# Outer products of a two-stream feed-forward block by seven block products, with two of the four weight sums made by accumulating DMAs

## The chip, the cores and the metric

The kernel runs on one core of one Trainium2 chip. The metric is the time of one execution on the device in microseconds (us), the median of a few runs. One further execution was taken by the hardware profiler, and all rows of a trace here are from that one. TensorE is called PE, VectorE DVE, ScalarE ACT, GpSimd POOL, SyncE SP.

## What is computed

The reference runs a first block (two layers of branches and a convolved feed-forward on `x`, 256 tokens of 1024), and then a second block of two layers on two streams, `x` and a context `c` of 256 tokens each. The change is in the second block's feed-forward half-steps:

```python
def modulate(h, m, i):
    return h * (1.0 + m[:, 3 * i + 1][:, None]) + m[:, 3 * i][:, None]

def ffn_half_step(s, m, i, norm_g, w_in, w_out):
    h = modulate(rmsnorm(s, norm_g), m, i)
    gu = h @ w_in
    y = (jax.nn.silu(gu[..., :D_FF]) * gu[..., D_FF:]) @ w_out
    return s + 0.5 * gate(m, i) * y
...
for l in range(DEPTH):
    m_x = modulation(c, w_mod[l], b_mod[l])
    m_c = modulation(c_ctx, w_mod[l], b_mod[l])[None]
    xs = ffn_half_step(xs, m_x, 0, ffn1_norm[l], ffn1_w_in[l], ffn1_w_out[l])
    cs = ffn_half_step(cs, m_c, 0, ffn1_norm[l], ffn1_w_in[l], ffn1_w_out[l])
    ...
    xs = ffn_half_step(xs, m_x, 2, ffn2_norm[l], ffn2_w_in[l], ffn2_w_out[l])
    if not last:
        ...
        cs = ffn_half_step(cs, m_c, 2, ffn2_norm[l], ffn2_w_in[l], ffn2_w_out[l])
```

Both streams go through the same weights, with D_FF = 2816. So three of the four half-steps work on two streams; the last one (layer 1, second half-step) on `x` alone. Between the half-steps of a layer lies a mixer with latent attention. The modulation is a product of a condition vector with 72 columns of 128 per layer.

## The kernel before, in words

All is float32. A matrix product is made of three float32r matmuls: each operand is split into a high part (a cast on ACT, L298) and the rest (a subtraction on DVE, L299), and `mm3` (L303 to L305) adds high by high, high by low and low by high into one PSUM bank. Tokens are the columns of a matmul (512 for both streams, 256 for one), weights are the stationary 128x128.

`ffn2` is a half-step. D_FF is cut into KF = 22 column blocks `j` of 128. For each, gate and up are made from one 512 KB weight tile each (8 blocks of the inner dimension, `times`), then silu and product, and the split of the result into an `r4` tile `g`. It works in two halves of 11 column blocks: after each half the down projection runs over the 8 output columns `d`, with one weight tile of 6 blocks (384 KB) and one of 5 (320 KB), and `gated_add` (L1086) adds the result, times the modulation's gate, to the residual `xs` or `cs`.

To start a half-step without waiting for its norm, the kernel makes the first column pairs from operands without the root: `ahead` (L1041, L1042) splits the residual times gain column by column as the gated additions finish, `firsts` multiplies them (and a 2-column bias, hence 258 columns), and `rooted` (L1067, L1070) multiplies the result by the root R afterwards. Layer 0's first half-step does this otherwise: there `h2` prepares the context ahead, and `first_two` makes its first pair. `streams` makes h from R for the remaining column blocks (two three-operand forms a block and stream, L1013 and L1016).

The modulation is made on DVE: `mod_step` loads a column block of its weights into `wm` (512 KB, two buffers) and multiplies it by the condition (L468, one for each stream). The products are kept in a queue `self.mods`; the calls `mod_step(n)` take n of them at a place in the program, and `mod_in`, `mod_out` are deadlines, which take all that a half-step's gains (or gates) need. In `ffn2` the calls stand behind the gate and up products and the loads of the down projection.

Loads are issued by SP. Buffers: `raw` 4 of 1024, `whi` and `wlo` 4 each, `r4` 15, `r4b` 4, PSUM 4 banks `ps`, 2 `sc`, 2 `tp`. The order within an engine comes from the tile framework that builds the program; each engine runs its own in order.

In the profile the names of tiles begin with the phase: `dn` in layer 0's first half-step of the second block, `lat` to `wa` in the mixer, `wo` from the mixer's output projection on and in the half-steps behind it.

## Time and profile before

| | before |
|---|---|
| median of 3 runs | 2477.66 us (2476.97 to 2477.69) |
| profiled execution | 2476.86 us |
| its span, first to last instruction | 2475.1 us |
| PE busy | 2456.9 us (99%), mean granted clock 0.999 |
| DVE busy | 1812.9 us (73%), 3180 instructions |
| ACT busy | 1197.4 us (48%), 2084 instructions |
| POOL busy | 1.2 us, 14 instructions |
| DMA | 395.91 MB, mean 160 GB/s |

A busy share is an average over the whole span. The section of rows below shows the same in slices and in windows; a row of a timeline gives the start, the duration, the engine, the line, and what the engine waited for before it. Instructions on DVE and ACT overlap by some 0.08 us, so that the distance between two starts, not the duration, is what an instruction takes of its engine.

### The profile page before, as it was taken

How to read it: one execution, taken by the hardware profiler on the slowest of the kernel's cores; microseconds unless marked ns; L12 is line 12 of the kernel's file. 1: busy time of each engine (PE TensorE's matmuls, PEld its weight loads, DVE VectorE, ACT ScalarE, POOL GpSimd, SP SyncE). 2: the span in 40 equal slices, each digit the busy share in tenths (PEclk: the TensorE clock that was granted, in tenths of full speed). 3: DMA queues.
4: the chain of work that ended last, by engine and by line, in shares of the span. 5: the costliest groups of instructions: out<-in, count | busy, mean ns of one | idle time of the engine just before them, and what ended most of it. 6: DMA issues, size and time to landing. Idle time of an engine off the chain costs nothing.

```text
span 2475.1 us, 39396 instructions
## 1 busy us (share of the span) xinstructions
PE 2456.9 (99%) x15211; PEld 2170.2 (88%) x15211; DVE 1812.9 (73%) x3180; ACT 1197.4 (48%) x2084; POOL 1.2 (0%) x14
## 2 busy tenths in 40 slices
PE   8999999999999999999999999999999999999998
...
DVE  8888887988998886776757875655765643688654
...
GB/s 251 172 156 181 199 183 235 183 152 172 216 215 205 202 197 149 211 182 125 115 59 42 120 147 127 177 145 125 123 147 163 244 153 74 91 117 139 178 206 120
DMA packets 123851, 395.91 MB, mean 160 GB/s; under 512 B 14352, under 2 KB 17168, under 8 KB 123408
## 3 DMA queue, kind: packets, MB, share of 16 engines
...
HBM read 392.30 MB, written 1.05 MB: 159 GB/s over the span
## 4 chain that ended last, share of the span: by engine, by line
PE 95%; DVE 2%; ACT 1%; DMA 0%; issue 0%; SPq 0%; DVEq 0%; ACTq 0%
PE wops L305 13%; PE wops L303 13%; PE wops L304 13%; PE dnps L304 6%; PE dnps L305 6%; PE dnps L303 6%; PE upps L305 3%; PE upps L303 3%; PE upps L304 3%; PE qkvps L304 1%; PE qkvps L305 1%; PE qkvps L303 1%; PE cvps L303 1%; PE cvps L305 1%; PE cvps L304 1%; PE latps L304 1%
## 5 line engine op out<-in xcount | busy, mean ns | idle before, releaser
L298 ACT CAST wowhi<-woraw 128x1024 fp32r<-128x1024 f32 (+3 forms) x266 | 246.4, 928 | 581.9 <-PE wops L304 359.6
L305 PE MATMUL wops<-wor,wowlo 128*128 128x512 f32 (+2 forms) x1371 | 480.5, 351 | 0.0
L303 PE MATMUL wops<-wor,wowhi 128*128 128x512 f32 (+2 forms) x1371 | 478.9, 350 | 0.0
L304 PE MATMUL wops<-wor,wowhi 128*128 128x512 f32 (+2 forms) x1371 | 478.6, 349 | 0.0
L299 DVE TENSOR_TENSOR wowlo<-woraw,wowhi 128x1024 fp32r<-128x1024 f32 (+3 forms) x266 | 283.9, 1071 | 216.9 <-ACT wowhi L298 208.7
L304 PEld LDWEIGHTS wops<-wor,wowhi 128*128 128x128 f32 x1371 | 258.0, 188 | 38.0 <-DVE wor L1042 0.2
L305 PEld LDWEIGHTS wops<-wor,wowlo 128*128 128x128 f32 x1371 | 257.9, 188 | 36.5
L303 PEld LDWEIGHTS wops<-wor,wowhi 128*128 128x128 f32 x1371 | 257.5, 188 | 36.5
L298 ACT CAST dnwhi<-dnraw 128x768 fp32r<-128x768 f32 (+2 forms) x144 | 125.1, 871 | 290.7 <-PE dnps L304 184.6
L299 DVE TENSOR_TENSOR dnwlo<-dnraw,dnwhi 128x768 fp32r<-128x768 f32 (+2 forms) x144 | 143.8, 1000 | 69.5 <-ACT dnwhi L298 66.9
L305 PE MATMUL upps<-hr,upwlo 128*128 128x256 f32 x656 | 183.2, 280 | 1.5 <-DVE upwlo L299 1.5
L304 PE MATMUL upps<-hr,upwhi 128*128 128x256 f32 x656 | 183.9, 281 | 0.0
L303 PE MATMUL upps<-hr,upwhi 128*128 128x256 f32 x656 | 183.8, 280 | 0.0
L468 DVE SCALAR_TENSOR_TENSOR dnjunk<-dnwm,cond 128x1024 bf16<-128x1024 f32 x134 | 163.5, 1220 | 2.9 <-DMA dnwm<-in_wm 1.7
L305 PE MATMUL dnps<-dnr,dnwlo 128*128 128x512 f32 (+1 forms) x371 | 142.4, 384 | 0.0
L304 PE MATMUL dnps<-dnr,dnwhi 128*128 128x512 f32 (+1 forms) x371 | 142.2, 383 | 0.0
L303 PE MATMUL dnps<-dnr,dnwhi 128*128 128x512 f32 (+1 forms) x371 | 142.1, 383 | 0.0
L468 DVE SCALAR_TENSOR_TENSOR wojunk<-wowm,cond 128x1024 bf16<-128x1024 f32 x114 | 138.9, 1219 | 0.0
L305 PEld LDWEIGHTS upps<-hr,upwlo 128*128 128x128 f32 x656 | 123.2, 188 | 2.3 <-DVE upwlo L299 2.3
L303 PEld LDWEIGHTS upps<-hr,upwhi 128*128 128x128 f32 x656 | 123.6, 188 | 0.0
L304 PEld LDWEIGHTS upps<-hr,upwhi 128*128 128x128 f32 x656 | 123.1, 188 | 0.0
L1127 DVE TENSOR_TENSOR wof<-wof,wops 128x512 f32<-128x512 f32 (+1 forms) x59 | 35.5, 602 | 110.2 <-PE wops L305 110.2
...
## 6 DMA issues: line engine op xcount, KB each, us to landing
woraw<-in_w2u SPq DMA_DIRECT2D x132, 512.0 KB, 3.7
upraw<-in_w1u SPq DMA_DIRECT2D x82, 512.0 KB, 4.3
wowm<-in_wm SPq DMA_DIRECT2D x73, 512.0 KB, 4.4
dnwm<-in_wm SPq DMA_DIRECT2D x67, 512.0 KB, 4.2
dnraw<-in_w2u SPq DMA_DIRECT2D x44, 512.0 KB, 4.2
...
woraw<-in_w2d SPq DMA_DIRECT2D x48, 320.0 KB, 2.9
qkvraw<-in_w1q SPq DMA_DIRECT2D x24, 512.0 KB, 4.4
```

The source lines that it names most:

```text
L298: act = self.nc.scalar.copy(hi, src)
L299: return act, self.nc.vector.tensor_tensor(lo, src, hi, ALU.subtract)
L303: mm(ps, L[0], R[0], start=st, stop=False)
L304: mm(ps, L[0], R[1], start=False, stop=False)
L305: mm(ps, L[1], R[0], start=False, stop=sp)
L468: nc.vector.scalar_tensor_tensor(junk, self.wm, 1.0, self.cond[:, s, :], ALU.mult, ALU.mult, accum_out=self.M[l][s][step][:, j:j + 1])
L1127: nc.vector.tensor_tensor(s, s, pss[1], ALU.mult)
```

## The change

The three half-steps on two streams go from `ffn2` to a new `ffn2s`; `ffn2` keeps the last one. In `ffn2s` two column blocks are made by `firsts` and `rooted`, in layer 0's first half-step too (`ahead` now prepares both streams there). The other 20 are made by seven products in Strassen's manner (Winograd's form): for one column block the matrix of weights has two rows, gate and up, and two halves of the inner dimension, and the matrix of activations has these halves and the two streams. `sums` makes seven activation operands once per half-step. `seven` makes seven weight operands of 4 blocks each. Each of the seven products is 4 blocks x 3 matmuls of 256 columns, 84 in all, where 48 of 512 columns stood.

Two of the four sums of weights are additions on DVE (L1161). The others are accumulating DMAs from HBM, issued by POOL: `es` is first loaded with half of up (SP), and the other half is added to it; gate's first half is added to the raw up tile. Each moves 256 KB; there are 120.

The down projection runs over three chunks of 8, 7 and 7 column blocks (`CHUNKS`), with one weight tile of 1024 or 896 a column, so that there are three rounds of `gated_add`. The modulation products stand elsewhere: one per column block from the seventh on, `mod_gate` per output column in the first chunk, two per column in the second, one in the third, and new calls in the mixer: one or two behind each product of `proj`, and one per output column of its projections (`mix2`). `r4b` has 8 buffers, `es` 2 of 1024, and `rope2`, `K2` and `Q2` live in `r4b` tiles.

```diff
-NU = {(0, 2): 2, (1, 0): 2, (1, 2): 3}
+NU = 2
+CHUNKS = ((0, 8), (8, 15), (15, 22))
...
+    def sums(self, Rs, more):
...
+        def h(out, s, k):
+            nc.vector.scalar_tensor_tensor(out, X[s][:, k, :], self.A[s][:, k:k + 1], Rs[s], ALU.mult, ALU.mult)
+            nc.scalar.activation(out, out, AF.Identity, bias=self.B[s][:, k:k + 1])
...
+        for k in range(4):
...
+            h(c1, 1, k)
+            h(f[:, T:], 1, k + 4)
+            nc.vector.tensor_tensor(t3, f[:, T:], c1, ALU.subtract)
+            h(f1[:, :T], 0, k)
+            nc.vector.tensor_tensor(f1[:, T:], f1[:, :T], c1, ALU.subtract)
+            two(f1, "x1", "t1")
+            nc.vector.scalar_tensor_tensor(f[:, :T], f1[:, T:], -1.0, f[:, T:], ALU.mult, ALU.subtract)
+            two(f, "t2", "c2")
+            f1 = self.f2()
+            h(f1[:, :T], 0, k + 4)
+            nc.vector.scalar_tensor_tensor(f1[:, T:], f[:, :T], -1.0, f1[:, :T], ALU.mult, ALU.subtract)
+            two(f1, "x2", "t4")
...
+    def seven(self, gate, up):
...
+        r1, r2 = self.raw(gate), self.raw(up)
+        h = slice(0, 4), slice(4, 8)
+        s = self.t("es", [P, 1024], 2, pool=self.p_second).rearrange("p (a b) -> p a b", a=8)
...
+        add = lambda o, a, b: nc.vector.tensor_tensor(o, a, b, ALU.add)
+        split(r1, "11", "12")
+
+        nc.sync.dma_start(s[:, h[1]], up[:, h[0]])
+        nc.gpsimd.dma_start(s[:, h[1]], up[:, h[1]], accum_op=ALU.add)
+        nc.gpsimd.dma_start(r2[:, h[0]], gate[:, h[0]], accum_op=ALU.add)
+        add(s[:, h[0]], s[:, h[1]], r1[:, h[0]])
+        split(s, "s2", "s1")
+        split(r2, "s3", "22")
+        add(r1[:, h[1]], s[:, h[0]], r1[:, h[1]])
+        split(r1[:, h[1]], "s4")
...
+    def begin(self, gate, up):
...
+        self.product(r1, W["11"], "x1", True, False)
+        m1 = self.f1()
+        nc.scalar.copy(m1, r1)
+        r2 = self.ps()[:, :T]
+        self.product(r2, W["12"], "x2", True, True)
+        u["y"] = self.f2()
+        nc.vector.tensor_tensor(u["y"][:, :T], m1, r2, ALU.add)
+        nc.scalar.activation(u["y"][:, :T], u["y"][:, :T], AF.Silu)
...
+    def middle(self, u, between):
...
+        self.product(r1, W["s2"], "t2", False, False)
+        u["u2"] = self.f1()
+        nc.scalar.copy(u["u2"], r1)
+        between()
+        u["r3"] = r3 = self.psc()[:, :T]
+        self.product(r3, W["s1"], "t1", True, False)
+        self.product(r1, W["s3"], "t3", False, False)
+        u["u3"] = self.f1()
+        nc.scalar.copy(u["u3"], r1)
+        nc.vector.tensor_tensor(u["u3"], u["u3"], r3, ALU.add)
...
+    def ffn2s(self, l, step, Rs, tmore, gmore, n4):
...
+                if n or jj >= 6:
+                    self.mod_step(1)
+                if todo:
+                    todo.pop(0)()
+                self.middle(u, todo.pop(0) if todo else lambda: None)
...
+                if n == 0:
+                    self.mod_gate(l, step, d)
+                elif n == 1:
+                    self.mod_step(2)
+                elif d < 5:
+                    self.mod_step(1)
...
@@ def mix2
+                pss.append(self.times(a["w2i"][l, 2 * c + i], [[x[:, :n] for x in y] for y in h], n))
+                self.mod_step(1 if c < 4 else 2, (l, 2, 16))
...
             W = self.weights_half(a["w2o"][l, d, :, 0:4])
+            self.mod_step(1, (l, 2, 16))
```

Engine DVE, in a column block's period of the new loop (L304 is the split's subtraction, L1161 a sum of weights, L473 a modulation product, `upes` the tile `es`; L1190 and L1206 to L1222 empty PSUM):

```order
L1161 TENSOR_TENSOR upraw_12567<-upes_12571,upraw_12567 128x512
L1161 TENSOR_TENSOR upes_12705<-upes_12705,upraw_12701 128x512
L1190 TENSOR_TENSOR upf_12621<-upf_12606,upps_12608 128x256
L304 TENSOR_TENSOR upwlo_12585<-upraw_12569,upwhi_12584 128x1024
L304 TENSOR_TENSOR upwlo_12590<-upraw_12567,upwhi_12589 128x512
L473 SCALAR_TENSOR_TENSOR upjunk_12626,M_131<-upwm_12624,cond 128x1024
L1215 SCALAR_TENSOR_TENSOR upf_12489<-upps_12461,upf_12489 128x256
L1220 TENSOR_TENSOR upf_12489<-upf_12519,upsc_12538 128x256
L304 TENSOR_TENSOR upwlo_12707<-upraw_12701,upwhi_12706 128x1024
L1222 SCALAR_TENSOR_TENSOR upf_12489<-upf_12563,upf_12489 128x256
L304 TENSOR_TENSOR upwlo_12715<-upes_12705,upwhi_12714 128x1024
L304 TENSOR_TENSOR upr4b_12566<-upf_12489,upr4b_12566 128x512
```

The pattern repeats every 13 rows: the next row adds the `es` tile of the second row into `upraw`, as the first row here does for the tile before it.

Engine DVE, around the gated additions of the mixer's output projection in layer 0, before (L1086 is `gated_add`, L316 the sum of squares of the norm, L1042 `ahead`):

```order
L1086 SCALAR_TENSOR_TENSOR xs<-wops_15503,hdMG_14504,xs 128x256
L1086 SCALAR_TENSOR_TENSOR cs<-wops_15503,hdMG_14506,cs 128x256
L299 TENSOR_TENSOR wowlo_15638<-woraw_15635,wowhi_15637 128x512
L316 TENSOR_TENSOR woS_15417<-woS_15417,wonq_15517 128x256
L1042 SCALAR_TENSOR_TENSOR wor_15520<-xs,woMA_15390,wor_15520 128x256
L316 TENSOR_TENSOR woS_15425<-woS_15425,wonq_15526 128x256
L1042 SCALAR_TENSOR_TENSOR wor_15520<-cs,woMA_15394,wor_15520 128x256
L1086 SCALAR_TENSOR_TENSOR xs<-wops_15537,hdMG_14504,xs 128x256
L1086 SCALAR_TENSOR_TENSOR cs<-wops_15537,hdMG_14506,cs 128x256
```

and now, at the same place (L1103 is `gated_add`, L473 a modulation product, L321 the sum of squares):

```order
L1103 SCALAR_TENSOR_TENSOR cs<-wops_16801,hdMG_15760,cs 128x256
L473 SCALAR_TENSOR_TENSOR wojunk_16686,M_132<-wowm_16684,cond 128x1024
L321 TENSOR_TENSOR woS_16757<-woS_16757,wonq_16824 128x256
L473 SCALAR_TENSOR_TENSOR wojunk_16688,M_135<-wowm_16684,cond 128x1024
L1103 SCALAR_TENSOR_TENSOR xs<-wops_16835,hdMG_15758,xs 128x256
L473 SCALAR_TENSOR_TENSOR wojunk_16692,M_132<-wowm_16690,cond 128x1024
L321 TENSOR_TENSOR woS_16749<-woS_16749,wonq_16849 128x256
L473 SCALAR_TENSOR_TENSOR wojunk_16694,M_135<-wowm_16690,cond 128x1024
L304 TENSOR_TENSOR wor4b_16852<-woMb_16720,wor4b_16852 128x2
L1103 SCALAR_TENSOR_TENSOR cs<-wops_16835,hdMG_15760,cs 128x256
L473 SCALAR_TENSOR_TENSOR wojunk_16698,M_132<-wowm_16696,cond 128x1024
L321 TENSOR_TENSOR woS_16757<-woS_16757,wonq_16858 128x256
```

What moved: modulation products stand between the gated additions, 20 of them from the first gated addition of this projection's last part to the gains (`woMA`) of the next half-step; the three-operand forms of `ahead` (L1061) come behind them.

On PE 60 column blocks have 84 matmuls of 256 columns for 48 of 512. On the queues SP has 888 instructions for 851, POOL 139 for 19.

## Rows read from the trace of the kernel before

**Rows 1.** The page: busy tenths in 40 slices, and the chain that ended last.

```profile
PE   8999999999999999999999999999999999999998
...
DVE  8888887988998886776757875655765643688654
...
PE 95%; DVE 2%; ACT 1%; DMA 0%; issue 0%; SPq 0%; DVEq 0%; ACTq 0%
```

**Rows 2.** Windows of 50 us: PE, PEld, DVE, ACT, POOL busy (x instructions), PEclk, DMA share, GB/s.

```profile
850.00:900.00 50.00, 50.00 (x218) 40.45 (x217) 43.06 (x68) 14.26 (x19) 0.00 (x0) 1.00 0.74 228
1300.00:1350.00 50.00, 49.98 (x271) 40.12 (x270) 41.23 (x84) 33.71 (x81) 0.00 (x0) 1.00 0.14 43
1450.00:1500.00 50.00, 50.00 (x217) 40.34 (x216) 26.94 (x38) 14.15 (x18) 0.00 (x0) 1.00 0.48 146
2300.00:2350.00 50.00, 50.00 (x425) 50.00 (x424) 30.89 (x43) 23.44 (x38) 0.00 (x0) 1.00 0.58 182
```

**Rows 3.** Windows of 5 us around the start of layer 0's second half-step.

```profile
1395.00:1400.00 5.00, 5.00 (x24) 4.01 (x23) 5.00 (x12) 4.35 (x10) 0.00 (x0) 1.00 0.65 205
1425.00:1430.00 5.00, 5.00 (x45) 5.00 (x44) 5.00 (x16) 4.76 (x8) 0.00 (x0) 1.00 0.00 0
```

**Rows 4.** DVE timeline, 1380 to 1418 us: start, us, line, operation, [idle before].

```profile
1386.66 0.48 DVE L1086 SCALAR_TENSOR_TENSOR xs<-wops,hdMG,xs 128x256 f32<-128x256 f32 x1 [1.93 <-PE wops L305]
1387.06 0.48 DVE L1086 SCALAR_TENSOR_TENSOR cs<-wops,hdMG,cs 128x256 f32<-128x256 f32 x1
1387.45 0.68 DVE L299 TENSOR_TENSOR wowlo<-woraw,wowhi 128x512 fp32r<-128x512 f32 x1
1388.05 0.48 DVE L1042 SCALAR_TENSOR_TENSOR wor<-xs,woMA,wor 128x256 fp32r<-128x256 f32 x1
...
1390.85 0.42 DVE L316 TENSOR_TENSOR woS<-woS,wonq 128x256 f32<-128x256 f32 x1
1391.18 0.48 DVE L1042 SCALAR_TENSOR_TENSOR wor<-xs,woMA,wor 128x256 fp32r<-128x256 f32 x1
...
1414.30 2.35 DVE L299 TENSOR_TENSOR wowlo<-woraw,wowhi 128x1024 fp32r<-128x1024 f32 x2
1416.57 1.26 DVE L1016 SCALAR_TENSOR_TENSOR wor<-wof,woMb,wor 128x256 fp32r<-128x256 f32 x3
```

**Rows 5.** PE timeline, 1428 to 1434 us: first wide matmul behind the first pairs.

```profile
1430.79 0.39 PE L303 MATMUL wops<-wor,wowhi 128*128 128x512 f32 x1
```

**Rows 6.** PE timeline, 1798 to 1804 us: the same place in layer 1.

```profile
1802.17 0.40 PE L303 MATMUL wops<-wor,wowhi 128*128 128x512 f32 x1
```

**Rows 7.** The page, DMA issues: tile and source, count, KB each, us to landing.

```profile
wowm<-in_wm SPq DMA_DIRECT2D x73, 512.0 KB, 4.4
...
woraw<-in_w2d SPq DMA_DIRECT2D x48, 320.0 KB, 2.9
```

**Rows 8.** DVE timeline, 1140 to 1152 us: a modulation product and the row behind it.

```profile
1140.67 1.22 DVE L468 SCALAR_TENSOR_TENSOR dnjunk<-dnwm,cond 128x1024 bf16<-128x1024 f32 x1
...
1141.82 0.30 DVE L299 TENSOR_TENSOR dnr<-dnMb,dnr 128x2 fp32r<-128x2 f32 x3
```

**Rows 9.** DVE timeline, 826 to 836 us: the root of x, and the split behind it.

```profile
833.97 1.22 DVE L299 TENSOR_TENSOR dnwlo<-dnraw,dnwhi 128x1024 fp32r<-128x1024 f32 x1
```

**Rows 10.** PE timeline, 828 to 836 us: first matmul behind the first block.

```profile
830.58 0.47 PE L303 MATMUL dnps<-dnr,dnwhi 128*128 128x256 f32 x1
```

**Rows 11.** Modulation products by phase: duration ns min/median/max, first and last start.

```profile
L468 DVE SCALAR_TENSOR_TENSOR wojunk<-wowm,cond x114: 1216/1218/1222, 1433.6 to 2022.1; 128x1024 bf16<-128x1024 f32 x114
```

**Rows 12.** DVE timeline, 1778 to 1786 us: behind the second root of layer 1.

```profile
1783.16 2.35 DVE L299 TENSOR_TENSOR wowlo<-woraw,wowhi 128x1024 fp32r<-128x1024 f32 x2
```

**Rows 13.** The page: costliest group, ACT casts of weights; busy us, mean ns.

```profile
L298 ACT CAST wowhi<-woraw 128x1024 fp32r<-128x1024 f32 (+3 forms) x266 | 246.4, 928 | 581.9 <-PE wops L304 359.6
```

**Rows 14.** ACT timeline, 1386 to 1392 us: a cast of 512 and a form of 256.

```profile
1386.46 0.62 ACT L298 CAST wowhi<-woraw 128x512 fp32r<-128x512 f32 x1 [5.19 <-PE wops L304]
...
1387.50 0.49 ACT L1041 ACTIVATE wor<-xs,woMA 128x256 fp32r<-128x256 f32 x1
```

More of the change, by code (lines that the diff above doesn't have):

```diff
@@ L984, in ffn1 @@
                 self.mod_in(0, 0)
-                self.h_c = [self.r4(2, 512, more=k >= 4) for k in range(KD)]
+                for k in range(5):
+                    self.ahead(0, k, 0)
             ps = self.ps()[:, :T]
@@ L1001, in ffn1 @@
             self.add_x(st, d, ps)
+            if l == 1 and d >= 5:
+                self.ahead(0, d, 0)
             if d == 5:
@@ new lines, in product @@
+    def product(self, ps, W, B, st, sp):
+        for k in range(4):
+            self.mm3(ps, (W[0][:, k, :], W[1][:, k, :]), self.B7[B][k], st and k == 0, sp and k == 3, True)
+    def begin(self, gate, up):
+        nc = self.nc
+        u = {"W": self.seven(gate, up)}
+        W = u["W"]
+        u["r1"] = r1 = self.ps()[:, :T]
+        self.product(r1, W["11"], "x1", True, False)
[6 more added lines that the diff above has]
+        nc.scalar.activation(u["y"][:, :T], u["y"][:, :T], AF.Silu)
+        return u
@@ new lines, in ends, with first, second @@
+    def ends(self, u, out):
+        nc = self.nc
+        W, r1, r3, y = u["W"], u["r1"], u["r3"], u["y"]
+        def first():
+            self.product(r1, W["22"], "t4", False, True)
+            nc.vector.scalar_tensor_tensor(y[:, :T], r1, -1.0, y[:, :T], ALU.mult, ALU.mult)
+        def second():
+            self.product(r3, W["s4"], "c2", False, True)
+            c = y[:, T:]
+            nc.vector.tensor_tensor(c, u["u2"], r3, ALU.add)
+            nc.scalar.activation(c, c, AF.Silu)
+            nc.vector.scalar_tensor_tensor(c, u["u3"], -1.0, c, ALU.mult, ALU.mult)
+            self.parts(out[0], out[1], y)
+        return [first, second]
@@ L1113, in ffn2 @@
+        return Rs
+    def ffn2(self, l, step, R, nh, ng):
+        nc, a = self.nc, self.a
+        wu, wd = "w2u2", "w2d2"
+        nu = 3
+        self.phase = "e"
+        first = self.firsts(1, [a[wu][l, i] for i in range(2, 2 * nu)])
+        xs = [self.r4(2, 512, more=k >= nh) for k in range(KD)]
+        W = self.streams([R], (0,), xs, a[wu][l, 2 * nu])
+        h = [(x[:, 0, :T], x[:, 1, :T]) for x in xs]
+        out = {}
         for half in range(2):
@@ L1128, in ffn2 @@
                 else:
[L1129 to L1135 removed]
+                    s2 = self.f2()[:, :T]
@@ new lines, in ffn2 @@
+                    Ws.append((k0, k1, self.weights(a[wd][l, d, :, half * HF + k0:half * HF + k1, :])))
+                for k0, k1, W in Ws:
+                    for k in range(k0, k1):
+                        self.mm3(ps, (W[0][:, k - k0, :], W[1][:, k - k0, :]), g[k], k == 0, k == HF - 1)
+                if half == 1 and d:
+                    self.turn(d - 1)
+                self.gated_add(0, d, ps)
+                if half == 1:
+                    self.norm_add(out, d, KD, self.xs[:, d, :])
```

261 lines of the change are left out of this document (154 added, 107 removed).

## The prediction

> **What bounds the kernel now.** The page comes first: in the slices PE stands at 9 tenths almost from end to end, and the chain that ended last lies to 95% on PE [rows 1]. Then the windows: 50.00 us of 50 on PE at clock 1.00, at both of the kernel's matmul widths [rows 2]. So the kernel lasts as long as its matmuls, and a change pays by what it takes off PE, less whatever newly makes PE wait. DVE is the engine to watch. It is far from full in the middle of the blocks [rows 2], but where one block ends and the next begins it has nothing left: 5.00 of 5 us [rows 3]. The DVE timeline gives the prices there [rows 4], the PE timelines the moments at which PE has used up the work that it can do without DVE [rows 5, 6], the DMA table the landings [rows 7].
>
> **What comes off PE.** In 50 us PE starts 217 matmuls of 512 columns or 425 of 256 [rows 2]: 230.4 and 117.6 ns each. A column block of gate and up costs 2 x 8 x 3 = 48 of the wide ones now, 11.06 us; by seven products it costs 7 x 4 x 3 = 84 of the narrow ones, 9.88 us. That is 1.18 us for each of 3 x 20 blocks, 70.8 us. The down projection keeps its matmuls; the two unchanged first column pairs and the first block of layer 0, whose pair is now made with 258 columns, give back about 1.2 us. Gain: **69.6 us**.
>
> **The steady loop stays with PE, narrowly.** From [rows 4, 8] a split of 1024 costs DVE 1.135 us (two in 2.27), a 512 one 0.60, a 256 sum 0.33, a 256 three-operand form 0.40, a modulation product 1.15. A period (the first fence of the change) holds 3 x 1.135 + 4 x 0.60 + 2 x 0.33 + 2 x 0.40 + one of L1190 at 0.33 + 1.15 = 8.8 us of DVE against 9.88 of PE. The cover is about 1 us, and it is gone if DVE waits anywhere for ACT for longer; I book nothing here and keep it as a rival. The two other weight sums are off DVE: as DVE additions they would add 2 x 0.60, and 10.0 us would pass PE.
>
> **Accumulating DMAs.** No row has one. An es buffer is held from the addition that ends its fill (order row "L1161 upes") to the one that reads it last, 12 of 13 rows, about 9 us; then it is loaded (256 KB; 320 KB land in 2.9 us [rows 7]) and accumulated into. With two buffers all this must fit into two periods, 19.8 us: an accumulation may take 19.8 - 9 - 2.9 = 7.9 us before PE feels it. Lower bound of its landing: 2.9 us like the plain load. Upper bound: it reads the destination too, and if each of its parts went one behind the other at the price of 512 KB, 4.4 us [rows 7], it is 8.8. I take 4.4 us (as many bytes moved as in a 512 KB load), so it is hidden. In bandwidth a block moves 2.1 MB in 9.9 us, 212 GB/s, where 228 GB/s took a share of 0.74 [rows 2]; with the accumulated bytes counted twice it is 265, share 0.86.
> The Trainium skill speaks against issuing them from POOL: "SBUF — State Buffer", the warning on the "DVE blocks DMA" trap, says that descriptors for POOL's DMAs are not written while DVE runs a two-port form. By that rule the landing could pass 7.9 us and the sum would be that of the third rival; the same page, "Who interferes with whom", gives the two-port forms to copies and scalar forms, and the loop's DVE rows are sums and three-operand forms, so by it nothing is added. No run here shows either yet.
>
> **Where DVE now stops PE: the starts of the three blocks.** sums() costs DVE 16 x 0.40 (L1114) + 4 x (2 x 0.33 + 2 x 0.40 + 3 x 0.60 + 0.33) = 20.8 us, where the rows it replaces (h from 32 three-operand forms) cost 12.8. PE's cover are the first pairs: 192 matmuls of about 0.118, 22.7 us.
> (A) Layer 0, first half-step. R is there at 833.97 [rows 9]; DVE then does 2 splits of first weights 2.3, sums 20.8, evacuations and the split of the first seven-product weights about 5.2: 28.3 us, so 862.3. PE begins the pairs at 830.58 [rows 10] and has them done by 853.5. Wait: 9 to 11, I take **10 us**.
> (B) Layer 0, second half-step. Before, no modulation product lies in the output projection of the mixer: the first in that phase is at 1433.6 [rows 11]. Now 20 of them stand between the gated additions (third fence) that empty PSUM for PE, all due before the gains of the next block exist. From the first gated addition (1386.66 [rows 4]) DVE has: 20 x 1.15, 10 gated additions 3.9, 4 splits of 512 2.4, 8 norm sums 2.6, small ones 0.9 = 32.8; then 16 of L1061 6.4, 6 gated additions 2.4, 2 splits 2.3, norm chain about 4.1 = 15.2 to the second R; then 4 splits 4.5 and sums 20.8 = 25.3 to the evacuation for which PE waits. 73.3 us, until 1460.0; PE's own work there ends with the pairs at 1430.79 [rows 5]. Difference 29.2. The modulation weights come through two buffers: 2.3 us of use and 4.4 of landing [rows 7] per 2 products and buffer, 3.35 us a pair, just what DVE takes for a pair and its neighbours (3.28). So there is no slack for a late load; 29 to 36, I take **33 us**.
> (C) Layer 1, first half-step: R at 1783.16 [rows 12], 29.4 us as in A with one more split, 1812.6; the pairs end at 1802.17 [rows 6]. 10.4 and small gaps: **12 us** (10 to 13).
> (D) The modulation products inside the mixers' head stages, 9 in layer 0 and some 12 in layer 1, 1.15 each: DVE leaves 8.8 us in 50 there [rows 2], so 0 to 13; I take **6 us**.
> (E) Nine chunk ends instead of six half ends, and three ragged first blocks: 0 (nothing waits) to 13 (about 1 us each); **5 us**.
> Sum: -69.6 + 10 + 33 + 12 + 6 + 5 = -3.6. Against the profiled execution, 2476.86 us (span 2475.1, 0.8 below the median of the runs), that is **2473 us**. Bounds of the terms: 48 us of waits give 2455, 86 give 2493.
>
> **Rivals.**
> 1. The starts are covered better. DVE idles 1.93 us ahead of a gated addition even at 1386.66 [rows 4]; if the modulation products begin earlier and fill such holes, B shrinks to about 15 and A and C to 6 each, with D and E at nothing: -69.6 + 27 = -42.6, **2434 us**. For it: R, PSUM and weights are double-buffered. Against it: DVE at 5.00 of 5 already [rows 3].
> 2. The loop is paced by ACT and DVE. m1, u2 and u3 are copied by ACT out of the bank that PE fills again two products (2.8 us) later; behind two or three casts of 0.93 us in the same queue [rows 13] the copy is late, and the sums behind it. It decides once a period loses over 1.1 us of DVE's time, its whole cover; with 0.9 us beyond that, 57 x 0.9 = 51 on top: **2524 us**, slower. For: 8.8 of 9.88. Against: ACT's own sum per period, 3 casts of 1024, 2 of 512 and 5 forms of 256, is at most 3 x 0.93 + 2 x 0.62 + 5 x 0.49 = 6.5 of 9.88 [rows 13, 14].
> 3. The accumulations land late. From 7.9 us on each further one costs half a us per block (two buffers): at 10 us 57 x 1.05 = 60 on top, **2533 us**, slower. For: no such row exists. Against: 4.4 us for twice the bytes.
> 4. The products do not give 84 x 0.118, since each takes new weights and 12 matmuls only. Against it: the 425 starts in 50 us changed their weights too, 424 loads [rows 2]. Half of the gain kept in the loop would give 35 on top, 2508.
>
> **How the numbers follow.** 0.2%, 5 us, is about what a measurement can tell here, so "same" is 2472.7 to 2482.6 about the median. Forecast (waits of 48 to 86 us): chance 0.55, of which 0.28 below, 0.14 within, 0.13 above. Rival 1: 0.17, all faster. Rival 2: 0.10, rival 3: 0.14, rival 4: 0.03, nearly all slower (0.01 level): 0.26 slower. Beyond them 0.01 for slower still. Faster 0.28 + 0.17 = 0.45, same 0.14 + 0.01 = 0.15, slower 0.13 + 0.27 = 0.40. The range reaches to rival 1's value and to the foot of rivals 2 and 3: 2434 to 2522; for the forecast alone it is 2455 to 2493.
>
> **What would show it.** PE: 84 matmuls of 256 in 9.9 us with DVE near 8.8 in the same window; PE idle for about 10, 33 and 12 us at the three starts, released by DVE (L1089, L304 of the first seven products), and nearly none before in the mixer's output projection except behind L1103. Wrong: a period over 10.3 us (rivals 2, 3; the DMA landing under 7.9 us tells which), PE never idle for over 6 us at the starts (rival 1), or waits at D and E larger than at B.

## The result, and the profile after

The changed kernel takes 2503.99 us (median of 4 runs, 2501.97 to 2506.27), the kernel before 2477.47 beside it: 26.5 us slower, a ratio of 1.0108 (95% interval 1.009 to 1.0125). Its profiled execution has a span of 2501.7 us. The forecast was 2473 us, a little faster; the chance of slower had been put at 0.40. In this document the three starts are the places where a half-step on two streams goes over from its first column pairs to the seven products.

The page of the changed kernel: busy time of each engine, the slices, and the chain that ended last. They answer to [rows 1].

```profile
PE 2417.4 (97%) x17383; PEld 2241.1 (90%) x17383; DVE 2097.3 (84%) x3806; ACT 1394.4 (56%) x2494; POOL 105.1 (4%) x134
...
PE   8999999999999899999999689999989999989998
...
DVE  8889887978998887988869889788887889889754
...
PEclk9999999999999999999999799999999999999999
...
PE 81%; DVE 11%; DMA 5%; ACT 2%; issue 2%; SPq 0%; DVEq 0%; ACTq 0%; POOLq 0%; POOL 0%
```

PE is busy for 39.5 us less than before (2417.4 for 2456.9), and waits for 66 us more: 84.3 us of the span without a matmul, 18.2 before. The slices of PEclk (the clock granted to PE, in tenths of full speed) say something that the forecast had no term for: one stands at 7. DVE's share of the chain goes from 2% to 11%.

Where the time went is read from the PE timeline. A half-step, and a mixer, begins with the first matmul of its first column pairs (258 columns), and one row of that kind marks each border. The two of layer 0's first half-step, at its start and where the mixer begins:

```profile
831.72 0.47 PE L308 MATMUL fps<-dnr4b,dnwhi 128*128 128x258 f32 x1
...
1189.73 0.29 PE L308 MATMUL latps<-dnr,dnwhi 128*128 128x258 f32 x1
```

The durations between these borders (the first includes the first block; the last runs to the span's end), with three of the experiments below, in us:

| stretch | before | after | x1 | b1 | v2 |
|---|---|---|---|---|---|
| up to layer 0's mixer | 1201.5 | 1189.7 | 1189.1 | 1202.1 | 1192.4 |
| mixer, layer 0 | 203.2 | **234.9** | 206.6 | **224.2** | 211.0 |
| second half-step, layer 0 | 374.0 | 369.1 | 366.4 | 374.3 | 361.7 |
| first half-step, layer 1 | 370.5 | 360.2 | 360.3 | 370.5 | 363.3 |
| mixer, layer 1 | 126.7 | **144.8** | 127.5 | **142.0** | 126.9 |
| last half-step and end | 199.4 | 203.0 | 203.2 | 204.4 | 203.3 |

The three changed half-steps win 27 us together, and the two mixers, whose arithmetic is unchanged, lose 50.

The loop itself is what was forecast. Windows of 50 us in layer 0 and layer 1, which answer to the 1450 window of [rows 2] (same columns):

```profile
980.00:1030.00 50.00, 50.00 (x423) 49.86 (x422) 43.07 (x69) 29.98 (x50) 7.78 (x9) 1.00 0.76 198
1950.00:2000.00 50.00, 50.00 (x423) 49.98 (x422) 43.90 (x71) 30.13 (x51) 7.78 (x9) 1.00 0.77 207
```

PE is never idle; 423 matmuls in 50 us make 118.2 ns each, so 9.93 us for a column block where 11.06 stood. DVE has 43 of 50 us. The accumulating DMAs stand beside it and hold nothing up in these windows. The rows of the DMA table that answer to [rows 7]; the first is the plain load of the tile that the second accumulates into:

```profile
upes<-in_w2u SPq DMA_DIRECT2D x60, 256.0 KB, 3.2
upes<-in_w2u POOLq DMA_DIRECT2D x60, 256.0 KB, 6.0
upraw<-in_w2u POOLq DMA_DIRECT2D x60, 256.0 KB, 4.4
```

Now the waits. Windows of 5 us at the starts of the three half-steps, in the output projection of layer 0's mixer, and beside the heads of layer 1's mixer:

```profile
860.00:865.00 5.00, 1.24 (x4) 0.98 (x5) 4.98 (x12) 2.15 (x4) 0.00 (x0) 0.50 0.01 2
1400.00:1405.00 5.00, 1.19 (x2) 0.50 (x2) 5.00 (x10) 0.83 (x2) 0.00 (x0) 0.50 0.57 181
1405.00:1410.00 5.00, 0.77 (x2) 0.50 (x2) 4.92 (x11) 0.84 (x2) 0.00 (x0) 0.50 0.39 136
1410.00:1415.00 5.00, 0.00 (x0) 0.00 (x0) 5.00 (x11) 0.42 (x1) 0.00 (x0) 0.50 0.64 207
1460.00:1465.00 5.00, 0.88 (x4) 0.91 (x5) 5.00 (x14) 4.15 (x8) 0.00 (x0) 0.50 0.00 0
1820.00:1825.00 5.00, 1.73 (x6) 1.09 (x6) 4.98 (x16) 3.46 (x6) 0.00 (x0) 0.64 0.00 0
2230.00:2235.00 5.00, 2.93 (x12) 2.13 (x11) 4.69 (x8) 4.00 (x8) 0.00 (x0) 0.60 0.62 204
```

DVE is full or nearly so in every one of them, and PE's granted clock is 0.50 to 0.64 in them. In the output projection (1400 to 1415 us) PE works for 2 of 15 us. The DVE timeline there, with the rows that the three PE waits end on (the `cs` rows of L1103 and the split L304 at 1415.14):

```profile
1399.43 0.47 DVE L1103 SCALAR_TENSOR_TENSOR cs<-wops,hdMG,cs 128x256 f32<-128x256 f32 x1
1399.96 1.22 DVE L473 SCALAR_TENSOR_TENSOR wojunk<-wowm,cond 128x1024 bf16<-128x1024 f32 x1
...
1401.11 0.42 DVE L321 TENSOR_TENSOR woS<-woS,wonq 128x256 f32<-128x256 f32 x1
1401.44 1.22 DVE L473 SCALAR_TENSOR_TENSOR wojunk<-wowm,cond 128x1024 bf16<-128x1024 f32 x1
...
1405.71 0.48 DVE L1103 SCALAR_TENSOR_TENSOR cs<-wops,hdMG,cs 128x256 f32<-128x256 f32 x1
...
1415.14 0.69 DVE L304 TENSOR_TENSOR wowlo<-woraw,wowhi 128x512 fp32r<-128x512 f32 x1
```

and PE's timeline in the same stretch:

```profile
1400.05 0.77 PE L308 MATMUL wops<-hdr4b,wowhi 128*128 128x512 f32 x1 [5.25 <-DVE cs L1103]
...
1406.33 0.55 PE L308 MATMUL wops<-hdr4b,wowhi 128*128 128x256 f32 x1 [5.09 <-DVE cs L1103]
...
1415.88 0.79 PE L310 MATMUL wops<-hdr4b,wowlo 128*128 128x512 f32 x1 [8.78 <-DVE wowlo L304]
```

Between two gated additions DVE takes two modulation products (1.15 us each) and a norm sum. PE fills its PSUM banks and waits until a gated addition gives one back, or until a split of weights queued behind the products is done (8.78 us).

And the clock. The start of layer 0's first half-step on PE, at the end of the wait and some 4 us behind it:

```profile
864.52 0.58 PE L310 MATMUL upps<-tr,upwlo 128*128 128x256 f32 x1 [3.57 <-DVE upwlo L304]
864.90 0.41 PE L308 MATMUL upps<-tr,upwhi 128*128 128x256 f32 x1
865.11 0.41 PE L309 MATMUL upps<-tr,upwhi 128*128 128x256 f32 x1
...
869.13 0.28 PE L309 MATMUL upps<-tr,upwhi 128*128 128x256 f32 x1
869.25 0.28 PE L310 MATMUL upps<-tr,upwlo 128*128 128x256 f32 x1
```

The same matmul of 256 columns takes 0.213 us from start to start and then 0.12: PE comes out of the wait at its lower level (clock 0.50, 1.2 GHz) and runs so for 4.4 us more. Summed over windows of 1 us (PE's busy time, times the share of the clock that is missing, times 0.9, since 0.45 of the time is lost at half the clock), some 18 us of PE's time went this way in the whole kernel, and none before. "TensorE: Matmul & The Clock Gate" of the Trainium skill, in "Part 1: The HAM clock gate", says that an idle PE falls back to 1.2 GHz; these rows agree.

### The profile page after: what moved, and what is told of

Its sections match the earlier page's. It is cut to its first block, busy times and chain, and to the rows that moved or that the text cites. A ratio compares the mean times of both kernels' runs of the same rounds, so it can differ in the third digit from the quotient of the medians.

```text
span 2501.7 us, 45389 instructions
## 1 busy us (share of the span) xinstructions
PE 2417.4 (97%) x17383; PEld 2241.1 (90%) x17383; DVE 2097.3 (84%) x3806; ACT 1394.4 (56%) x2494; POOL 105.1 (4%) x134
## 4 chain that ended last, share of the span: by engine, by line
PE 81%; DVE 11%; DMA 5%; ACT 2%; issue 2%; SPq 0%; DVEq 0%; ACTq 0%; POOLq 0%; POOL 0%
PE upps L310 8%; PE upps L308 8%; PE upps L309 8%; PE dnps L308 6%; PE dnps L309 6%; PE dnps L310 6%; PE eps L310 2%; PE eps L308 2%; PE eps L309 2%; PE upsc L309 2%; PE upsc L310 2%; PE upsc L308 2%; DMA upes<-in_w2u 1%; DVE upwlo L304 1%; PE qkvps L309 1%
## 5 line engine op out<-in xcount | busy, mean ns | idle before, releaser
L303 ACT CAST upwhi<-upraw 128x1024 fp32r<-128x1024 f32 (+1 forms) x262 | 249.3, 951 | 224.8 <-PE upps L309 106.4
L304 DVE TENSOR_TENSOR upwlo<-upraw,upwhi 128x1024 fp32r<-128x1024 f32 (+1 forms) x262 | 283.4, 1098 | 42.4 <-ACT upwhi L303 40.9
L308 PE MATMUL upps<-tr,upwhi 128*128 128x256 f32 x1000 | 285.2, 285 | 14.4 <-DVE upf L1089 13.5
L310 PE MATMUL upps<-tr,upwlo 128*128 128x256 f32 x1000 | 284.0, 284 | 7.8 <-DVE upwlo L304 7.7
L309 PE MATMUL upps<-tr,upwhi 128*128 128x256 f32 x1000 | 283.0, 283 | 0.0
L308 PEld LDWEIGHTS upps<-tr,upwhi 128*128 128x128 f32 x1000 | 191.3, 191 | 18.9 <-ACT tr L303 10.3
L310 PEld LDWEIGHTS upps<-tr,upwlo 128*128 128x128 f32 x1000 | 191.1, 191 | 9.2 <-DVE upwlo L304 9.0
L309 PEld LDWEIGHTS upps<-tr,upwhi 128*128 128x128 f32 x1000 | 191.1, 191 | 0.3
L310 PE MATMUL dnps<-upr,dnwlo 128*128 128x256 f32 (+1 forms) x535 | 169.7, 317 | 0.0
L309 PE MATMUL dnps<-upr,dnwhi 128*128 128x256 f32 (+1 forms) x535 | 169.5, 317 | 0.0
L308 PE MATMUL dnps<-upr,dnwhi 128*128 128x256 f32 (+1 forms) x535 | 169.2, 317 | 0.0
L304 DVE TENSOR_TENSOR dnwlo<-dnraw,dnwhi 128x896 fp32r<-128x896 f32 (+3 forms) x146 | 150.1, 1030 | 22.0 <-ACT dnwhi L303 21.2
L473 DVE SCALAR_TENSOR_TENSOR dnjunk<-dnwm,cond 128x1024 bf16<-128x1024 f32 x120 | 146.0, 1217 | 6.9 <-DMA dnwm<-in_wm 6.6
L308 PE MATMUL dnps<-upr4b,dnwhi 128*128 128x512 f32 (+1 forms) x366 | 140.9, 387 | 0.7 <-ACT upr4b L303 0.7
L309 PE MATMUL dnps<-upr4b,dnwhi 128*128 128x512 f32 (+1 forms) x366 | 141.1, 385 | 0.0
```

Of the source, the lines that this page charges most:

```text
L303: act = self.nc.scalar.copy(hi, src)
L304: return act, self.nc.vector.tensor_tensor(lo, src, hi, ALU.subtract)
L308: mm(ps, L[0], R[0], start=st, stop=False, skip_group_check=skip)
L309: mm(ps, L[0], R[1], start=False, stop=False, skip_group_check=skip)
L310: mm(ps, L[1], R[0], start=False, stop=sp, skip_group_check=skip)
L473: nc.vector.scalar_tensor_tensor(junk, self.wm, 1.0, self.cond[:, s, :], ALU.mult, ALU.mult, accum_out=self.M[l][s][step][:, j:j + 1])
```

## The experiments

The theory was that the time is lost by the modulation products that the change moved into the mixers: DVE is late there, PE waits, and comes back at a low clock. In the trace of the changed kernel 62 products run inside the mixers (43 in layer 0, 19 in layer 1), where none ran before: 48 for the second half-steps, 14 for the mixers' own use. The first rival was that the accumulating DMAs land late, the second that DVE's total is the limit, wherever the products stand. Each run has a run of the kernel before beside it, on the same chip (2477.5 to 2478.0 us).

**x1, the mixers without the 48 products for the second half-steps.** They are left out of the computation with the loads of their weights; the other 14 stay.

```diff
@@ mod_step
                 l, step, j, s = self.mods.pop(0)
+                if step == 2 and upto[1:] == (2, 16):
+                    continue
```

> The changed kernel without the 48 modulation products that are taken inside the two mixers for the second half-steps (left out of the computation, with their loads; those gains are then zero plus bias). Theory (the modulation products put into the mixers make DVE late there and PE waits): some 45 us of DVE go from the mixers, the two mixer stretches lose most of the 44 us by which they grew, and the clock stays up there: 2455 to 2465 us. Rival (the accumulating DMAs are late and hold the loops up): the loops are untouched, at most 5 us less, 2499 us.

Measured: 2455.0 us (0.991, interval 0.9894 to 0.9927). That is 49 us less than the changed kernel, and 28 + 17 of them in the two mixers (table above), which are back at nearly their old lengths. The loops and the accumulations are as they were, so the first rival can't have been the main loss. By itself this run doesn't part the place of the products from their sum on DVE, which falls too (2097.3 to 2045.1 us busy); b1 does.

**b1, the kernel before with that part of the change alone.** `mod_step` in its feed-forward stops short of the second half-step's products, and the mixers take them at the places of the changed kernel.

```diff
@@ ffn2 of the kernel before
-                        self.mod_step(rate)
+                        self.mod_step(rate, (l, 2, 0) if step == 0 else (LAYERS,))
@@ mix2
+                self.mod_step(1 if c < 4 else 2, (l, 2, 16))
...
             W = self.weights_half(a["w2o"][l, d, :, 0:4])
+            self.mod_step(1, (l, 2, 16))
```

> The kernel before with one part of the change alone: the modulation products for the second half-steps are held back until the mixers, at the places of the changed kernel (32 in layer 0, of them 10 in its output projection, 16 in layer 1). Theory (place of the modulation products): the mixers grow by some 15 to 30 us, nothing else changes, 2493 to 2508 us. Rival (they hurt only together with the sums of the seven products): under 5 us, 2483 or less.

Measured: 2520.1 us (1.0173, interval 1.0158 to 1.0188), 42.7 us slower than the kernel before, more than expected. The products cost this with no seven products, no sums and no POOL DMA in the program: 21 us in the mixer of layer 0, 15 in that of layer 1, 5 in the last half-step, where 8 products now stand and none stood before. Two windows in its output projection:

```profile
1405.00:1410.00 5.00, 0.62 (x3) 0.19 (x2) 4.79 (x10) 1.16 (x3) 0.00 (x0) 0.97 0.63 192
1410.00:1415.00 5.00, 1.19 (x2) 0.50 (x2) 5.00 (x17) 3.51 (x9) 0.00 (x0) 0.50 0.42 125
```

DVE is nearly full, PE works for 1.8 of 10 us and the clock falls to half, with 10 products there where the changed kernel has 20. And the total of DVE did not grow: 72% of the span. The place of the work is enough, taken with its loads: no run moves the one without the other. In the changed kernel ACT waits 5.1 us in layer 1's mixer for weights of the projection and the half-step behind it, and none before, but no wait of PE over 0.25 us ends on one of those casts.

**x2, all four weight sums on DVE.**

```diff
-        nc.sync.dma_start(s[:, h[1]], up[:, h[0]])
-        nc.gpsimd.dma_start(s[:, h[1]], up[:, h[1]], accum_op=ALU.add)
-        nc.gpsimd.dma_start(r2[:, h[0]], gate[:, h[0]], accum_op=ALU.add)
+        add(s[:, h[1]], r2[:, h[0]], r2[:, h[1]])
+        add(r2[:, h[0]], r2[:, h[0]], r1[:, h[0]])
```

> The changed kernel with all four weight sums as additions on DVE and no accumulating DMA. Theory (accumulations are hidden, and DVE has 1.1 us of a 9.9 us period to spare): the two additions, 1.2 us per block, use the spare time up, the period goes from 9.94 to about 10.1 us where a modulation product stands in it, so 2505 to 2520 us. Rival (accumulations late): faster than the changed kernel by over 10 us, 2490 or less.

Measured: 2497.7 us (1.0082, interval 1.0067 to 1.0097), 6 us faster than the changed kernel. Both expectations are missed. The loop, in the window that answers to 980 to 1030 above:

```profile
980.00:1030.00 50.00, 50.00 (x424) 50.00 (x424) 48.33 (x78) 30.55 (x51) 0.00 (x0) 1.00 0.39 135
```

424 matmuls as before, DVE at 48.3 of 50: the two additions fit beside PE, and the period stays. So the accumulations save nothing in the loop, and cost a little somewhere else; v1 and v4 show where.

**x3 and x5, matmuls in the wait.** x3 has 75 and x5 33 matmuls of 128 columns on constants, at each start, between the first pairs and the seven products.

```diff
         self.sums(Rs, tmore)
+        fill = self.ptp()
+        for _ in range(NFILL):
+            nc.tensor.matmul(fill[:, :P], self.ones, self.ones, start=True, stop=True)
```

> The changed kernel with 75 further matmuls of 128 columns, on constants and read by nobody, on PE at the three starts, between the first column pairs and the first of the seven products. Theory (a PE that waits gets a lower clock, which then costs some 2.5 us per start): the waits are filled with 8 to 9 us of matmuls, the clock stays at 1.00 behind them, 2 to 7 us less, 2497 to 2502 us. Rival (the clock falls for another reason): no change or some us more.

Measured: 2523.3 us (1.0182, interval 1.0167 to 1.0197), 19 us slower; the run doesn't tell the two apart. The matmuls were twice as long as thought, 16.7 us at each start from the first to the last, 50 in all. As 19 us came of 50, the starts had held some 10 us each to be filled (wait and lower clock together). x5 has the right length:

> As the run with 75 further matmuls at each start, which took 16.7 us there, but with 33, so 7.3 us, about the length of the waits. Theory (a PE that waits gets a lower clock, which then costs some 2.5 us per start): 3 to 8 us faster than the changed kernel, 2496 to 2501 us. Rival (the clock falls for another reason): 2504 us or more.

Measured: 2500.4 us (1.0097, interval 1.008 to 1.0114), 3.6 us below the changed kernel: at the low end of the theory, and no more than the spread of the runs (2499.96 to 2504.03 beside 2501.97 to 2506.27), so it isn't clear of no gain. The window of x5 at the start of layer 0's first half-step:

```profile
860.00:865.00 5.00, 4.84 (x43) 4.63 (x42) 4.98 (x10) 1.69 (x4) 0.00 (x0) 1.00 0.00 2
```

At the same place where the changed kernel stood at 0.50, the clock is at 1.00, with some 7 us of matmuls that nobody reads. So the low clock does come from the wait.

**n3, a third column pair at the starts.** Its operands need no root; the first pair is emptied ahead of the sums, to make room in PSUM.

```diff
+        g0 = finish(0, 0)
+        pss = [self.ps() for _ in range(3)]
...
+        for i in range(2):
+            W = self.weights(a[wu][l, 4 + i])
...
         self.sums(Rs_in, tmore)
```

> The changed kernel with a third column pair made ahead of the root at the three starts (its evacuations put before the sums of the activations), so 19 instead of 20 column blocks by seven products. Theory (at the starts PE has nothing to do while DVE makes the sums, which costs some 10 us each with the low clock behind): PE gets 11.4 us of work more where it waited and does one block of 9.9 less, 8 to 9 us saved at each start, 2475 to 2485 us. Rival (the start is bound by DVE's total, and the third pair's own DVE work, 4 us, only moves the wait): under 3 us per start, 2495 us or more.

Measured: 2499.1 us (1.009, interval 1.0075 to 1.0105), 4.9 us less, 1.6 per start. The time is the rival's, its reason only in part: PE's waits at the three starts fall from 5.9, 8.4 and 7.3 us to 3.5, 3.7 and 4.4, some 10 us in all. The rest is behind the pair, and the pair costs PE about 1.5 us more than the block that it replaces (11.4 for 9.9), three times.

**p1, the two sums on POOL.** As x2, with `nc.gpsimd.tensor_tensor` for the two additions.

> The changed kernel with the two accumulating DMAs replaced by two additions of 128x512 on POOL. The earlier run with them on DVE was 6 us faster than the changed kernel. Theory (the accumulations are late at the chunk ends, by some 6 us in all): as good as on DVE or better, 2490 to 2498 us. Rival (POOL and DVE share access to the memory, and the additions slow DVE): over 2505 us.

Measured: 2520.9 us (1.0174, interval 1.0159 to 1.019), 17 us slower than the changed kernel and 23 slower than x2. The rival held. Rows of the DVE groups in 50 us of the loop, of x2 and of p1 (line, engine, operation, shapes, count, busy us, mean ns), and POOL's addition (duration in ns, minimum, median, maximum):

```profile
L1161 DVE TENSOR_TENSOR upes<-upes,upraw 128x512 f32<-128x512 f32 x5 | 3.4, 684 | 0.0
```

```profile
L304 DVE TENSOR_TENSOR upwlo<-upraw,upwhi 128x1024 fp32r<-128x1024 f32 x9 | 11.0, 1218 | 1.6 <-ACT upwhi L303 1.6
L1161 DVE TENSOR_TENSOR upes<-upes,upraw 128x512 f32<-128x512 f32 x5 | 7.8, 1555 | 0.0
```

```profile
L1164 POOL TENSOR_TENSOR upes<-upraw x60: 1285/1410/3731, 834.0 to 2108.8; 128x512 f32<-128x512 f32 x60
```

An addition of 128x512 takes DVE 0.685 us in x2, and 1.55 in the mean of p1's loop, beside POOL's of 1.41; those of p1 that ran beside none of POOL's took 0.69 us at most. "SBUF — State Buffer" of the Trainium skill, under "Who interferes with whom", says that a DVE instruction with two inputs in SBUF contends with one of POOL that reads SBUF; these rows agree. Most splits, which have two inputs too, kept their time because no addition of POOL ran beside them: of the 462 splits of 128x512, 128x896 and 128x1024 between 830 and 2110 us, 401 had none beside them, and not one of these was slower. Of the other 61, the 30 that began ahead of POOL's addition lost nothing, and 26 of the 31 that began while it ran took over 0.1 us longer, as the one of 128x512 at 991.61 us with 1.77 for 0.685.

**v1, the modulation products elsewhere, and the whole computation.** Six more in the first block, three a column in the first chunk's down projection, 22 called from the projections of layer 0's mixer, 4 left in its output projection, none in layer 1's mixer. None is called beside the heads, but they run there all the same: in the trace 18 stand 95 to 124 us behind the border of layer 0's mixer, and the first matmul of the heads (`hdps`) stands at 97.

```diff
@@ ffn2s
-                    self.mod_gate(l, step, d)
+                    left = len(self.mods)
+                    self.mod_gate(l, step, d)
+                    self.mod_step(max(0, 3 - left + len(self.mods)))
@@ mix2
-                self.mod_step(1 if c < 4 else 2, (l, 2, 16))
+                if l == 0:
+                    self.mod_step(2 if i == 0 else 4, (l, 2, 16))
...
-            self.mod_step(1, (l, 2, 16))
```

> The changed kernel with the whole computation and the modulation products elsewhere: six more in the first block, three a column in the first chunk's down projection, 22 in the projections of layer 0's mixer, none in layer 1's mixer and none beside the heads. Four are left in the output projection of layer 0. Theory (place of the modulation products): the mixers lose about 40 us of their growth, 2455 to 2470 us, below the kernel before. Rival (DVE's total is the limit, wherever they stand): they make PE wait in the chunks instead, 2495 us or more.

Measured: 2487.4 us (1.0039, interval 1.0026 to 1.0052), 16.6 less. Both sides are half right: layer 1's mixer is back at 126.9 us, layer 0's only at 219.0, and the half-steps are longer, that of layer 1 by 10.9. A chunk end there, of v1, on DVE and on POOL:

```profile
2042.89 0.69 DVE L1161 TENSOR_TENSOR upes<-upes,upraw 128x512 f32<-128x512 f32 x1 [2.31 <-DMA upes<-in_w2u]
```

```profile
2037.16 0.86 POOL L1165 DMA_DIRECT2D upes<-in_w2u  x1 [12.91 <-DMA upes<-in_w2u]
```

DVE's addition waits for the accumulated `es` tile. POOL issued the accumulation only at 2037.16, having waited 12.9 us for the plain load into that tile. SP had issued that load only at 2031.99, behind four loads of modulation weights that took its queue from 2021.68 to 2031.17. The accumulation landed 5.7 us after its issue. DVE's sum (L1190) was late by that, ACT waited 7.67 us for it, and its copy (L1199) gave PE back its bank. The PE row, and the clock in the two windows about it:

```profile
2045.82 0.58 PE L308 MATMUL upps<-tr,upwhi 128*128 128x256 f32 x1 [6.57 <-ACT upf L1199]
```

```profile
2040.00:2045.00 5.00, 0.00 (x0) 0.00 (x0) 2.69 (x6) 0.00 (x0) 0.00 (x0) 0.81 0.88 289
2045.00:2050.00 5.00, 4.18 (x20) 4.18 (x21) 3.48 (x6) 1.99 (x4) 0.86 (x1) 0.51 0.69 176
```

PE waited 6.57 us, and its granted clock in the window behind is 0.51.

**v2, as v1 with all sums on DVE** (the edit of x2), and ten more products in the first block.

> The whole computation, with the modulation products moved as in the run v1 (ten more of them in the first block, none beside the heads or in an output projection) and all four weight sums as additions on DVE. In v1 PE lost some 25 us behind chunk ends, where an accumulation landed late under three other loads. Theory (products out of the mixers, and no accumulation to wait for): these 25 us go, 2450 to 2468 us, below the kernel before. Rival (DVE, with 70 us more to do, is now the limit of the loops): 2480 us or more.

Measured: 2459.9 us (0.9929, interval 0.9914 to 0.9943), 44 us below the changed kernel and 17.7 below the kernel before. Windows in its output projection and beside the heads of layer 1:

```profile
1400.00:1405.00 5.00, 5.00 (x36) 4.60 (x35) 5.00 (x12) 4.06 (x10) 0.00 (x0) 1.00 0.56 202
2230.00:2235.00 5.00, 5.00 (x39) 4.49 (x37) 4.76 (x14) 4.06 (x15) 0.00 (x0) 1.00 0.17 53
```

PE is at 5.00 of 5 where the changed kernel had 1.19 and 2.93. The loops hold, with DVE at 88% of the span, more than in the changed kernel (84%): its total isn't the limit. Layer 0's mixer is still 7.8 us longer than before; 12 products run there 95 to 114 us behind its border, where the heads have begun.

**v4, v2 with the accumulating DMAs put back.**

> The run v2 (2459.9 us) with one part put back: the two weight sums by accumulating DMAs from POOL in place of the two additions on DVE. Theory (the accumulations land late behind chunk ends, where the modulation weights load too): 10 to 25 us above v2, 2470 to 2485 us. Rival (v1 lost its 25 us by the place of its modulation products, not by the DMAs): within 5 us of v2 or, with DVE relieved of 70 us, below it.

Measured: 2477.3 us (0.9995, interval 0.9986 to 1.0004), 17.4 us above v2, with DVE relieved of 69 us. The second half-step of layer 0 is 9.7 us longer, the first of layer 1 5.5. DVE waits for the accumulation 27 times, as this row of its waits says (total, times, longest):

```profile
DVE upes L1161 <- DMA upes<-in_w2u: 52.3, 27, 3.8
```

With v1 and x2 this settles the DMAs: they are hidden while the loads run ahead, cost 6 us as the change has them, and 17 with the modulation loads placed as in v2.

**v3 and v5, what is left at the starts.** v3 is v2 with the short fill, v5 is v2 with the third pair.

> The same with 33 further matmuls, read by nobody, on PE at each of the three starts, as in the short fill, which gave 3.6 us. Theory (a waiting PE gets a lower clock): 2 to 6 us below the run v2 beside it. Rival: no difference, or slower, since the waits are shorter here than 7.3 us.

> The run v2 with the third column pair of the run n3, which gave 5 us on the changed kernel. Theory (what is left at the three starts is DVE's sums of activations, and PE has too little to do beside them): 3 to 10 us below v2, 2450 to 2457 us. Rival (DVE's own extra work for the pair moves the wait): no difference.

Measured: 2460.8 us (0.9937, interval 0.992 to 0.9953) and 2460.7 (0.9932, interval 0.9916 to 0.9949). Neither is told from v2. In v3 the mean granted clock is 0.999 for v2's 0.993, and yet no time is won. At layer 1's start the fill takes 7.5 us where v2 waits for 4.1, so matmuls that outlast a wait are part of it; the rest isn't told by these runs.

## Why the prediction was wrong, step by step

The kernel was forecast at -69.6 + 66 = -3.6 us and came out at +26.5. By its terms, with the stretches of the table and a gain of 22.4 us for each half-step (20 blocks of 11.06 - 9.94 us); a stretch has its chunk ends in it, so A and C hold a share of E:

- **What comes off PE: 69.6 forecast, 67 measured.** The period is 9.93 to 9.98 us, not 9.88. Right.
- **The steady loop stays with PE.** Right, and with more room than was said: x2 put another 1.2 us on DVE without a longer period. The hand sum was somewhat too high: 8.8 us a period, and 10.0 with the two additions, where 43.07 and 48.33 of 50 us make 8.6 and 9.6 in a period of 9.93. So "10.0 us would pass PE" was wrong.
- **Accumulating DMAs hidden.** 4.4 us had been taken, and 4.4 and 6.0 us to landing were measured, below the 7.9 that two buffers allow. Right in the loop, not everywhere: x2 shows 6 us of cost. The third rival's mechanism exists, but not for its reason: not the accumulation is slow, the plain load ahead of it is late in SP's queue (v1, v4). The trap that "SBUF — State Buffer" of the Trainium skill warns of made no difference that these runs show: with DVE at 43 of 50 us the landing stayed at 4.4 and 6.0 us.
- **A, 10 us.** From the end of the first block to the mixer: 831.72 to 1189.73, 358.0 us, where it was 830.58 [rows 10] to 1201.5, 370.9. It won 12.9 of 22.4, so 9.5 were lost. The size is right, the working isn't: its own figures gave 862.3 - 853.5 = 8.8 us of wait, 10 was taken, and PE stood idle for 5.9 (1.57 + 0.46 + 0.29 + 3.57). About 2.7 more are the lower clock behind it.
- **B, 33 us.** The output projection of layer 0's mixer ran from 1380.28 to 1424.61, 44.33 us, where it had run from 1383.66 to 1404.63, 20.97; the first pairs behind it lasted until 1464.12, 39.51 us, where they had lasted until 1430.79 [rows 5], 26.16. That is 23.4 and 13.3: 36.7 us lost. Right in its place, its cause and nearly in its size. PE's waits are 29.6 us of it (19.1 in the output projection, 2.1 at the norm, 8.4 at the start); the lower clock is about the rest.
- **C, 12 us.** 22.4 - 10.3 = 12.1. The size is right; the waits at the start are 7.3 us, and the lower clock behind them some 2.7.
- **D, 6 us (0 to 13): the step that failed.** The mixers outside layer 0's output projection lost 31.7 - 23.4 + 18.1 = 26.4 us (the table's differences, less what B has). That is over the term's upper bound. It counted "9 in layer 0 and some 12 in layer 1", 21 products, where the trace has 21 and 19 in these stretches, 14 of them for the mixers' own use. And it set their 1.15 us against DVE's free time, as if only its share counted: "DVE leaves 8.8 us in 50 there". But beside the heads DVE is a link of a chain in which each step waits for the one before on another engine: scores (PE), their maximum (DVE L1640), exponential (ACT L1646), reciprocal of the sum (DVE L1647), scaling (ACT L1650), transposition (PE L1659). So are the splits of the heads' operands (DVE L304). The fences below show a product ahead of a split, one ahead of a reciprocal and one ahead of a maximum. b1 shows the price with no other part of the change: 15 us in layer 1's mixer from 16 products, 18 us of DVE.
- **E, 5 us.** 22.4 - 4.9 for layer 0's second half-step, less the 13.3 that B has, leaves 4.2. Right. Not in the sum: 3.6 us in the last half-step, where 8 modulation products now stand and none stood before (b1, with 8 there, loses 5.0), and 1.1 in the first block.

The timelines of DVE, ACT and PE beside the heads of layer 1, of the changed kernel:

```profile
2223.05 1.23 DVE L473 SCALAR_TENSOR_TENSOR cvjunk<-cvwm,cond 128x1024 bf16<-128x1024 f32 x1 [1.47 <-DMA cvwm<-in_wm]
...
2224.20 0.42 DVE L304 TENSOR_TENSOR hdr4b<-hdf,hdr4b 128x256 fp32r<-128x256 f32 x1
...
2228.61 1.22 DVE L473 SCALAR_TENSOR_TENSOR cvjunk<-cvwm,cond 128x1024 bf16<-128x1024 f32 x1 [0.47 <-DMA cvwm<-in_wm]
...
2229.76 0.16 DVE L1647 RECIPROCAL hdsm<-hdsm 128x2 f32<-128x2 f32 x1
...
2231.75 1.21 DVE L473 SCALAR_TENSOR_TENSOR cvjunk<-cvwm,cond 128x1024 bf16<-128x1024 f32 x1
...
2232.89 0.68 DVE L1640 TENSOR_REDUCE hdnm<-hdsc 128x1 f32<-128x512 f32 x1
```

```profile
2221.61 0.41 ACT L303 CAST hdr4b<-hdf 128x256 fp32r<-128x256 f32 x1 [0.97 <-DVE hdf L1507]
...
2229.95 0.72 ACT L1650 ACTIVATE hdes<-hdes,hdsm 128x512 f32<-128x512 f32 x1 [0.82 <-DVE hdsm L1647]
```

```profile
2224.67 0.73 PE L310 MATMUL hdsc<-latr4b,hdr4b 128*128 128x512 f32 x2 [1.16 <-DVE hdr4b L304]
...
2236.24 0.47 PE L1659 MATMUL hdtp<-ident,hdes 128*128 128x128 f32 x1 [3.17 <-ACT hdes L1650]
```

The split at 2224.20 could have begun when ACT's cast (2221.61, 0.41 us) was done; it stands behind the product of 2223.05, which itself had held DVE's queue for 1.47 us, as its weights had not landed, and PE waits 1.16 us for the split. The reciprocal at 2229.76 stands behind the product of 2228.61, and ACT waits 0.82 us for it. PE's longest wait here, 3.17 us, ends on a scaling whose chain has the maximum of 2232.89 in it, which stands behind the product of 2231.75. The products waited for their weights in this mixer five times:

```profile
DVE cvjunk L473 <- DMA cvwm<-in_wm: 5.7, 5, 2.9
```

Of the 18.1 us of this mixer 10 are waits of PE (11.2 us without a matmul, 1.2 before) and some 3 the clock; how the rest falls isn't told by these views.

The sum of all terms, 9.5 + 36.7 + 12.1 + 26.4 + 4.2 + 3.6 + 1.1 - 67.2, is 26.4 us (measured: 26.5). So 20 of the 30 us of error lie in D, 4 in B, 4 in the last half-step, 2 in the gain. The low clock, 18 us, has no line of its own here: it is inside A to D. That A to C came out right with no term for it is in part luck: their waits were put too long (10, 33 and 12 us for 5.9, 29.6 and 7.3), and the clock made up for it. The sign that was named, PE idle for about 10, 33 and 12 us at the starts, was therefore not met at A and C.

The range (2434 to 2522) held the time, but not by its working: the forecast's own bounds were 2455 to 2493, and the part from there to 2522 was there for rivals 2 and 3, a loop paced by DVE and ACT and accumulations that land late in it. Neither happened in the loop (423 matmuls in 50 us). What was given too little weight is that neither bound of D had a row behind it that shows a product beside the heads.

## What to carry to other kernels

Work that fills an engine's idle time must be placed where that engine is not a link of a chain: 48 modulation products of 1.15 us cost next to nothing in the feed-forward and 36 us inside the mixers (b1), at the same share of busy time. If an edit frees one engine by loading another, look first at the stretches that hold no slack for the second, not at the loop. And a sum moved from a busy engine to a DMA is only worth it where that engine is the limit: here it wasn't, and the DMA brought a load order that could be late.

## What the runs showed that had not been expected

- Behind the wait at the first start PE ran on at its lower level for 4.4 us (0.213 us for a matmul of 256 columns, then 0.12), and in the output projection it stood at 0.50 in all three windows from 1400 to 1415 us, in which it worked for 2 of 15 us. In all some 18 us of PE's time went that way. Filling the waits kept the clock at 1.00 there and gave 3.6 us in x5, not clear of the spread, and nothing in v3.
- An addition of 128x512 on POOL takes 1.41 us and stretches an addition on DVE that runs beside it from 0.685 us: the mean in the loop is 1.55. Who begins first decides: a split that began ahead of POOL's addition lost nothing.
- The version that beats both kernels, v2 at 2459.9 us, does the seven products with no accumulating DMA and keeps the modulation products out of layer 1's mixer and of both output projections; 12 still run beside the heads of layer 0. The three starts still lose some 7 to 11 us each there, wait and lower clock together; neither a third pair nor a fill won them back; fewer DVE instructions in the sums weren't tried.
